# A kernel of four layers on one core: the expert part's gate multiplications spread one per step, and their tiles loaded on the weights' queue

## The chip, the cores and the metric

The kernel runs on one core of a Trainium2 chip. The time is what the device takes for one launch, in microseconds; of several runs the median counts. Lower is better.

## What is computed

Two blocks run one after the other on 256 tokens of width 1024. The first block has two layers of convolution, retention and window attention. The second has two layers of a mixer and a feed-forward part that looks up experts. The change lies in that last part alone, so only it is shown (the two layers are called layer 0 and layer 1 below):

```python
def block(t):
    q = (t @ w_pq).reshape(T, PEER_HEADS, 2, PEER_HALF)
    s = jnp.einsum('thpk,hpnk->thpn', q, sub_keys, ...)
    ...
    gate = jax.nn.softmax(best_s, axis=-1)
    u = expert_down[experts]
    act = jax.nn.gelu(jnp.einsum('td,thkd->thk', t, u, ...), approximate=False)
    wgt = (gate * act).astype(t.dtype)
    vv = expert_up[experts]
    return jnp.einsum('thk,thkd->td', wgt, vv)
```

There are 16384 experts, and each token uses 128 of them. The kernel does not gather. It multiplies the tokens with all experts, and the gate, which is zero for all others, picks.

## The kernel before

The experts are worked in 64 blocks `b2` of 256. For each, `down(b2, dst)` computes the activations of all tokens (16 key steps, three matmuls each, since every f32 operand is split in a high and a low part), and the loop `for b2 in range(64)` near the end of `peer` multiplies them with the rows of `up`: 24 matmuls of 128x512 (line 1184) for each step, summed over all steps in four PSUM banks, `accs`. I call one pass of that loop a step, and the loop the up part.

The weights of a step come as two halves. `half` (lines 100 to 115) loads each on SP's queue into one of four buffers `raw` (512 KB), ACT rounds it into `hi`, and DVE subtracts that, into `lo`; `hi` and `lo` have five buffers each. The activations of a step are split in the same way, into `wah` on ACT and `wal` on DVE, with two buffers each. So DVE has two `lo` and one `wal` for each step.

The gates come from an earlier loop. For the first 24 of 128 key columns (steps 0 to 11) they are multiplied there into `acti`. For the rest they are written to DRAM, `g_dram`, in 13 tiles of 1 MB; each serves four steps. `late(b2)` fetches a tile every fourth step, on ACT's queue, into one of two buffers `gt`, and multiplies the step's activations with it on DVE (line 1147). For steps 12 to 43 the activations lie ready in SBUF (`saved`: the tiles `uh`, `ul`, `xs`, `actl`); from step 44 on `late` also calls `down`, which loads 1 MB more and has 48 matmuls of 128x256. `late(b2 + AHEAD)`, with AHEAD = 2, stands in step `b2`.

Layer 0 also computes the modulation of the mixer that follows it, in units `ada`: a load of 256 KB on SP's queue into one of two buffers, and a multiplication with a sum on DVE (line 298), with a short addition (line 300). They begin at step 16. Seventeen have come due by then; after that there is one for each step, and four from step 44 on. Layer 1 has none.

The program text doesn't set the order on an engine. A scheduler does, by what it expects to be ready when, with the program's order and priorities; SP's queue, DVE, ACT and PE then each take their instructions strictly in that order. `tc.issue_after(x)` binds what a block issues on the engine of `x` to come behind `x` there.

Of the kernel before, what the change touches and what calls it, by code (L numbers as in the profile page):

```python
# [8 lines left out]
F32 = mybir.dt.float32  # L9
# [10 lines left out]
P = 128  # L20
T = 256
# [11 lines left out]
PEER_NS, PEER_NI, AHEAD = 44, 12, 2  # L33
# [17 lines left out]
def two_blocks_kernel(ctx: ExitStack, tc: tile.TileContext, ins: dict, out: bass.AP, stages=None):  # L51
    nc = tc.nc
# [30 lines left out]
    def nm(base):  # L83
        uid[0] += 1
        return f"{base}_{uid[0]}"

    def split(hi, lo, src):
        return nc.scalar.copy(hi, src), nc.vector.tensor_tensor(lo, src, hi.bitcast(F32), op=ALU.subtract)  # L88
# [4 lines left out]
    def bank(ring="mm", shape=(P, 2, T)):  # L93
        n = turns[ring] = turns.get(ring, -1) + 1
        b = BANKS[ring][n % len(BANKS[ring])]
        return psum.tile(list(shape), F32, tag=f"bank{b}", name=nm(ring))

    after = [None, None, 0]
    last_dma = [None]
# [14 lines left out]
    def slab(src):  # L114
        h = [half(src, i) for i in range(2)]
        return [[x[k] for x in h] for k in range(2)]
# [107 lines left out]
    def shift_bias(pb, pool, w, sh2):  # L224
        for ct in range(2):
            for kt in range(KT):
                for i in range(2):
                    nc.tensor.matmul(pb[0:2, 0, ct * P:(ct + 1) * P], sh2[:, kt, :], w[i][ct][:, kt * P:(kt + 1) * P],
                                     start=kt == 0 and i == 0, stop=kt == KT - 1 and i == 1)
        row = pool.tile([2, T], F32, tag="sbr", name=nm("sbr"))  # L230
        nc.scalar.copy(row, pb[0:2, 0, :])
        for ct in range(2):
            nc.tensor.matmul(pb[:, 1, ct:ct + 1], row[:, ct * P:(ct + 1) * P], ones_c[0:2, :], start=True, stop=True)
        b = pool.tile([P, 2], F32, tag="sb", name=nm("sb"))
        nc.vector.tensor_copy(b, pb[:, 1, 0:2])
        return b
# [17 lines left out]
    if stages_m:  # L254
        tb_dram = [drp.tile([P, 383], F32, tag=f"tb{h}", name=f"tb{h}") for h in range(8)]
        x_dram = [drp.tile([P, KT, T], F32, tag=f"xd{i}", name=f"xd{i}") for i in range(DEPTH)]
        g_dram = [drp.tile([13, P, T, 8], F32, tag=f"gd{i}", name=f"gd{i}") for i in range(DEPTH)]
# [24 lines left out]
    def ada_units(l, pool, tag, bufs, size, place=None):  # L282
        cact = []

        def load():
            cp, ct = place or (pool, "c_rows")
            cact.append(cp.tile([P, D], F32, tag=ct, name=nm("c_rows"), bufs=1))
            nc.sync.dma_start(cact[0], ins["c_rows"])
            nc.scalar.activation(cact[0], cact[0], AF.Silu)

        yield load
        for j in range(48):
            for c in range(0, D, size):
                def unit(j=j, c=c):
                    w = pool.tile([P, size], F32, tag=tag, name=nm("ada"), bufs=bufs)
                    nc.sync.dma_start(w, ins["w_ada"][l, j, :, c:c + size])
                    t = pool.tile([P, 1], F32, tag="adt", name=nm("adt"))
                    nc.vector.scalar_tensor_tensor(w, w, 1.0, cact[0][:, c:c + size], op0=ALU.mult, op1=ALU.mult,  # L298
                                                   accum_out=t)
                    nc.vector.tensor_tensor(mods[l][:, j:j + 1], mods[l][:, j:j + 1], t, op=ALU.add)  # L300
                yield unit
# [648 lines left out]
    def peer(l, uu, follow):  # L950
        NS, NI = PEER_NS, PEER_NI
        GS = 2 * NI
        NGR = (P - GS) // 8
        with ExitStack() as bx:
# [13 lines left out]
            def down(b2, dst):  # L968
                w = slab(ins["down"][l, b2])
                ps = bank("pm")  # L970
                mm_T(ps, w, hh)
                nc.scalar.activation(dst, ps, AF.Gelu)  # L972

            with ExitStack() as tx:
# [14 lines left out]
                with tc.tile_pool(name=f"tt{l}", bufs=2) as tq:  # L989
                    for h in range(8):  # L990
                        w = slab(ins["w_pq"][l, h])
                        qT = tq.tile([P, 2, T], F32, tag="qT", name=nm("qT"))
                        if h < PEER_U:
                            pb = bank("pb")
                            b = shift_bias(pb, tq, w, shifts["p", l])
# [36 lines left out]
                def saved(i):  # L1032
                    t, k = (spare[i // 4], i % 4) if i < 12 else (actl, i - 12)
                    return t[:, 2 * k:2 * k + 2, :]
# [57 lines left out]
            wu = bx.enter_context(tc.tile_pool(name=f"up{l}", bufs=2))  # L1092
# [37 lines left out]
                    nc.scalar.dma_start(g_dram[l][:NGR, :, t0:t0 + 16, :].rearrange("g p t b -> p g t b"), stg)  # L1130

            accs = [bank("acc", (P, 512)) for _ in range(4)]
            gtile = None
            wa_q = {}

            def late(b2):
                nonlocal gtile
                if b2 < NS:
                    wa = saved(b2 - NI)
                else:  # L1140
                    wa = wu.tile([P, 2, T], F32, tag="ua", name=nm("wa"), bufs=4)
                    down(b2, wa)
                if (2 * b2 - GS) % 8 == 0:
                    gtile = wu.tile([P, T, 8], F32, tag="gt", name=nm("gt"), bufs=2)
                    nc.scalar.dma_start(gtile, g_dram[l][(2 * b2 - GS) // 8])
                g = gtile[:, :, 2 * b2 % 8:2 * b2 % 8 + 2].rearrange("p t b -> p b t")
                nc.vector.tensor_tensor(wa, wa, g, op=ALU.mult)  # L1147
                wa_q[b2] = wa

            units = ada[follow[1]] if follow else []  # L1150
            credit, pace = 0, None
            for b2 in range(64):
                if follow and b2 == NI + 4:
                    units.extend(ada_units(follow[1], wu, "ud", 2, 512, (upool, "uh")))
                credit += PEER_ADA[b2 >= NS]
                while units and credit >= 1:
                    credit -= 1
                    with ExitStack() as es:
                        if PACE and pace:
                            es.enter_context(tc.issue_after(pace.ins))  # L1160
                        if PACE > 1:
                            es.enter_context(tc.issue_after(last_dma[0].ins))
                        units.pop(0)()
                if b2 == NS:
                    X[0] = glob.tile([P, KT, T], F32, tag="xT", name=nm("xT"))
                    for k2 in range(KT // 2):
                        nc.sync.dma_start(X[0][:, 2 * k2:2 * k2 + 2, :], x_dram[l][:, 2 * k2:2 * k2 + 2, :])
                for b in range(NI, 64) if b2 == 0 else ():
                    if b < AHEAD:
                        late(b)  # L1170
                if NI <= b2 + AHEAD < 64:
                    late(b2 + AHEAD)
                wa = acti[:, 2 * b2:2 * b2 + 2, :] if b2 < NI else wa_q.pop(b2)
                uh, ul = slab(ins["up"][l, b2])
                wah = wu.tile([P, 2, T], F32R, tag="ub", name=nm("wah"), bufs=2)
                wal = wu.tile([P, 2, T], F32R, tag="uc", name=nm("wal"), bufs=2)
                pace = split(wah, wal, wa)[1]
                for k in range(2):
                    first, end = b2 == 0 and k == 0, b2 == 63 and k == 1
                    for tt in range(2):  # L1180
                        tsl = slice(tt * P, (tt + 1) * P)
                        for lh, rh, i in ((wah, uh, 0), (wah, ul, 1), (wal, uh, 2)):
                            for n in range(2):
                                nc.tensor.matmul(accs[2 * tt + n], lh[:, k, tsl],  # L1184
                                                     rh[k][:, n * 512:(n + 1) * 512],
                                                     start=first and i == 0, stop=end and i == 2)
# [18 lines left out]
    for i in range(nh, len(stages)):  # L1205
        k, l = stages[i]
        u = (mix if k == "m" else peer)(l, u, follows[i])
# [147 lines left out]
```

## Time and profile before

| | |
|---|---|
| Median of 3 runs | 3028.61 us (3024.74 to 3031.89) |
| The profiled execution's own time | 3032.76 us |
| Its span in the profile | 3030.4 us |
| PE busy | 2939.5 us, 97% of the span |
| DVE busy | 2418.9 us, 80% |
| ACT busy | 1521.7 us, 50% |
| Moved by DMA | 598.59 MB, mean 198 GB/s |
| Up part of layer 0, first to last 128x512 matmul | from 1562.2 us, some 490 us |
| Up part of layer 1 | from 2549.1 to 3021 us |

The profile is of one execution. Matmuls overlap in their pipeline, so that "PE busy" reaches 100% wherever they follow each other without a gap, and gaps are better seen by counting the matmuls of a stretch. A wait is put down to the instruction whose signal came last.

### The profile page before, as it was taken

To read this page: it belongs to the slowest core of one execution; us is meant where nothing else is said; L and a number is where in the kernel's file an instruction comes from. 1 tells how busy PE (TensorE), PEld (TensorE's weight loads), DVE (VectorE), ACT (ScalarE), POOL (GpSimd) and SP (SyncE) were. 2 spreads that over 40 slices of the span, in tenths; PEclk is the share of its full clock that TensorE was granted. 3 is DMA by queue.
4 is the path that set the end of the run, shared out by engine and by line. 5 is a ranking of instruction groups with operands and counts; after the bars stand their busy time and mean duration, and the time that the engine had idled before them with its cause. 6 is when DMAs were issued, how large, how long until landed. Compare 5 with 4: busy or idle time off the path is not lost.

```text
span 3030.4 us, 55658 instructions
## 1 busy us (share of the span) xinstructions
PE 2939.5 (97%) x21784; PEld 2726.1 (90%) x21784; DVE 2418.9 (80%) x5084; ACT 1521.7 (50%) x2113; POOL 76.3 (3%) x92
## 2 busy tenths in 40 slices
PE   8999999999999998999999899999999999999999
PEld 7889999988999997999987689888899999788998
DVE  7899988888898676999878767767699997855565
ACT  5664535565454554555544444445355444444443
POOL 0000000000000000000000000000000000000000
PEclk8999999999999999999999999999899999999999
DMA  6357448434745552556677878864255677765664
GB/s 205 123 181 265 165 161 278 162 124 161 241 168 169 175 165 93 178 178 208 214 244 275 274 242 273 279 221 152 84 169 182 202 218 238 272 208 194 204 218 136
DMA packets 227065, 598.59 MB, mean 198 GB/s; under 512 B 24881, under 2 KB 85841, under 8 KB 223473
## 3 DMA queue, kind: packets, MB, share of 16 engines
q1 hardware_dynamic: 160080, 533.63, 52.9%
q10 hardware_dynamic: 66720, 61.39, 6.3%
q8 instruction: 171, 2.80, 0.4%
q14 instruction: 94, 0.76, 0.1%
HBM read 562.97 MB, written 31.98 MB: 196 GB/s over the span
## 4 chain that ended last, share of the span: by engine, by line
PE 61%; DVE 6%; DMA 6%; issue 2%; ACT 1%; ACTq 0%; DVEq 0%
PE acc L1184 15%; PE pm L125 8%; PE pm L126 8%; PE pm L127 8%; DMA ada<-in_w_ada_dram 4%; PE mm L125 3%; PE mm L127 3%; PE g L1119 3%; PE mm L126 3%; DVE lo L88 2%; DVE actl L1147 1%; PE mm L137 1%; PE mm L136 1%; DVE ada L298 1%; PE mm L135 1%
## 5 line engine op out<-in xcount | busy, mean ns | idle before, releaser
L88 ACT CAST hi<-raw 128x1024 fp32r<-128x1024 f32 x904 | 946.6, 1050 | 993.6 <-PE pm L126 251.6
L88 DVE TENSOR_TENSOR lo<-raw,hi 128x1024 fp32r<-128x1024 f32 x904 | 1115.5, 1237 | 303.2 <-ACT hi L88 300.2
L125 PE MATMUL pm<-h_hi,hi 128*128 128x256 f32 x2272 | 642.2, 283 | 10.8 <-ACT acti L972 7.7
L126 PE MATMUL pm<-h_lo,hi 128*128 128x256 f32 x2272 | 640.4, 282 | 4.5 <-DVE h_lo L219 4.5
L127 PE MATMUL pm<-h_hi,lo 128*128 128x256 f32 x2272 | 639.9, 282 | 2.9 <-DVE lo L88 2.9
L125 PEld LDWEIGHTS pm<-h_hi,hi 128*128 128x128 f32 x2272 | 430.1, 189 | 13.2 <-ACT acti L972 8.1
L126 PEld LDWEIGHTS pm<-h_lo,hi 128*128 128x128 f32 x2272 | 430.2, 189 | 6.4 <-DVE h_lo L219 4.9
L127 PEld LDWEIGHTS pm<-h_hi,lo 128*128 128x128 f32 x2272 | 430.1, 189 | 3.6 <-DVE lo L88 3.5
L125 PE MATMUL mm<-h_hi,hi 128*128 128x256 f32 x1472 | 419.5, 285 | 0.0
L126 PE MATMUL mm<-h_lo,hi 128*128 128x256 f32 x1472 | 416.0, 283 | 0.0
L127 PE MATMUL mm<-h_hi,lo 128*128 128x256 f32 x1472 | 415.6, 282 | 0.0
L1184 PE MATMUL acc<-hi,wal 128*128 128x512 f32 x1024 | 318.7, 394 | 25.5 <-DVE wal L88 25.5
L1184 PE MATMUL acc<-lo,wah 128*128 128x512 f32 x1024 | 318.0, 391 | 3.9 <-DVE lo L88 3.9
L1184 PE MATMUL acc<-hi,wah 128*128 128x512 f32 x1024 | 317.7, 392 | 0.0
L125 PEld LDWEIGHTS mm<-h_hi,hi 128*128 128x128 f32 x1472 | 278.5, 189 | 8.9 <-issue 8.3
L126 PEld LDWEIGHTS mm<-h_lo,hi 128*128 128x128 f32 x1472 | 278.6, 189 | 6.2 <-issue 6.1
L127 PEld LDWEIGHTS mm<-h_hi,lo 128*128 128x128 f32 x1472 | 278.3, 189 | 5.6 <-issue 5.6
L1184 PEld LDWEIGHTS acc<-hi,wal 128*128 128x128 f32 x1024 | 191.9, 189 | 73.4 <-DVE wal L88 33.9
L420 DVE SCALAR_TENSOR_TENSOR conv<-cv,conv_dw,conv 128x256 f32<-128x256 f32 x480 | 241.0, 512 | 3.3
L1184 PEld LDWEIGHTS acc<-lo,wah 128*128 128x128 f32 x1024 | 192.8, 189 | 46.4 <-DVE lo L88 5.6
L1184 PEld LDWEIGHTS acc<-hi,wah 128*128 128x128 f32 x1024 | 190.4, 189 | 38.1 <-ACT wah L88 0.3
L298 DVE SCALAR_TENSOR_TENSOR ada<-ada,c_rows 128x512 f32<-128x512 f32 (+1 forms) x144 | 126.2, 881 | 77.4 <-DMA ada<-in_w_ada_dram 71.9
(400 smaller groups left out, 4731.7 us busy)
## 6 DMA issues: line engine op xcount, KB each, us to landing
raw<-in_w_in_dram SPq DMA_DIRECT2D x264, 512.0 KB, 4.1
raw<-in_down_dram SPq DMA_DIRECT2D x256, 512.0 KB, 4.3
raw<-in_up_dram SPq DMA_DIRECT2D x256, 512.0 KB, 4.6
gd<-stg ACTq DMA_DIRECT2D x32, 832.0 KB, 5.0
gt<-gd ACTq DMA_DIRECT2D x26, 1024.0 KB, 6.7
ada<-in_w_ada_dram SPq DMA_DIRECT2D x48, 512.0 KB, 4.9
ada<-in_w_ada_dram SPq DMA_DIRECT2D x96, 256.0 KB, 4.2
raw<-in_w_ret_out_dram SPq DMA_DIRECT2D x32, 512.0 KB, 3.6
```

The costliest lines, as they stand in the source:

```text
L88: return nc.scalar.copy(hi, src), nc.vector.tensor_tensor(lo, src, hi.bitcast(F32), op=ALU.subtract)
L125: nc.tensor.matmul(ps[:, ct, :], wh[:, kt, c], ah[:, kt, :], start=s, stop=False)
L126: nc.tensor.matmul(ps[:, ct, :], wh[:, kt, c], al[:, kt, :], start=False, stop=False)
L127: nc.tensor.matmul(ps[:, ct, :], wl[:, kt, c], ah[:, kt, :], start=False, stop=e)
L135: nc.tensor.matmul(ps[:, tt, :], ah[:, kt, c], wh[:, kt % 4, :], start=kt == 0, stop=False)
L136: nc.tensor.matmul(ps[:, tt, :], ah[:, kt, c], wl[:, kt % 4, :], start=False, stop=False)
L137: nc.tensor.matmul(ps[:, tt, :], al[:, kt, c], wh[:, kt % 4, :], start=False, stop=kt == KT - 1)
L298: nc.vector.scalar_tensor_tensor(w, w, 1.0, cact[0][:, c:c + size], op0=ALU.mult, op1=ALU.mult, accum_out=t)
L420: nc.vector.scalar_tensor_tensor(a, v[:, k:k + T], dw[:, c, k:k + 1], a, op0=ALU.mult, op1=ALU.add)
L1119: nc.tensor.matmul(pg[:, k, :], oh[0][:, j // 2, :, j % 2], oh[2 + i][:, j // 2, :, j % 2], start=i == 0, stop=i == 2)
L1147: nc.vector.tensor_tensor(wa, wa, g, op=ALU.mult)
L1184: nc.tensor.matmul(accs[2 * tt + n], lh[:, k, tsl], rh[k][:, n * 512:(n + 1) * 512], start=first and i == 0, stop=end and i == 2)
```

## The change

Three things. The gate tiles are loaded by `gate_columns(n)` on SP's queue, tied behind the load of the half before it; tile n is asked for in step 8 + 4n, four steps ahead of the first step that needs it. The multiplication of step `b2 + 2` is tied on DVE behind the `wal` of step `b2 - 1`. The loop `for b in range(NI, 64) if b2 == 0`, which did nothing with these constants, is gone.

```diff
             accs = [bank("acc", (P, 512)) for _ in range(4)]
-            gtile = None
+            gtiles = {}
             wa_q = {}
 
+            def gate_columns(n):
+                gtiles[n] = wu.tile([P, T, 8], F32, tag="gt", name=nm("gt"), bufs=2)
+                nc.sync.dma_start(gtiles[n], g_dram[l][n])
+
             def late(b2):
-                nonlocal gtile
                 if b2 < NS:
                     wa = saved(b2 - NI)
                 else:
                     wa = wu.tile([P, 2, T], F32, tag="ua", name=nm("wa"), bufs=4)
                     down(b2, wa)
-                if (2 * b2 - GS) % 8 == 0:
-                    gtile = wu.tile([P, T, 8], F32, tag="gt", name=nm("gt"), bufs=2)
-                    nc.scalar.dma_start(gtile, g_dram[l][(2 * b2 - GS) // 8])
-                g = gtile[:, :, 2 * b2 % 8:2 * b2 % 8 + 2].rearrange("p t b -> p b t")
+                g = gtiles[(2 * b2 - GS) // 8][:, :, 2 * b2 % 8:2 * b2 % 8 + 2].rearrange("p t b -> p b t")
                 nc.vector.tensor_tensor(wa, wa, g, op=ALU.mult)
                 wa_q[b2] = wa
...
-                for b in range(NI, 64) if b2 == 0 else ():
-                    if b < AHEAD:
-                        late(b)
+                n, c = divmod(2 * (b2 + AHEAD + 2) - GS, 8)
+                if b2 and 0 <= n < NGR and c == 0:
+                    with tc.issue_after(last_dma[0].ins):
+                        gate_columns(n)
                 if NI <= b2 + AHEAD < 64:
-                    late(b2 + AHEAD)
+                    with tc.issue_after(wsplit.ins):
+                        late(b2 + AHEAD)
...
-                pace = split(wah, wal, wa)[1]
+                wsplit = pace = split(wah, wal, wa)[1]
```

What it moves is seen in the order of each engine. On DVE, in layer 0, before, the stretch that begins with the `lo` of step 2 (L1147 is a gate multiplication, `x4` four of them in a row; `uh` and `ul` are the saved activations of steps 12 to 15 and 16 to 19; `wal_19805` is step 2's and `wal_19845` step 3's):

```order
L88 TENSOR_TENSOR lo_19794<-raw_19792,hi_19793 128x1024
L88 TENSOR_TENSOR lo_19800<-raw_19798,hi_19799 128x1024
L1147 TENSOR_TENSOR uh_15557<-uh_15557,gt_20112 128x512 x4
L88 TENSOR_TENSOR wal_19805<-acti_14594,wah_19804 128x512
L88 TENSOR_TENSOR lo_19834<-raw_19832,hi_19833 128x1024
L1147 TENSOR_TENSOR ul_15558<-ul_15558,gt_20278 128x512 x4
L88 TENSOR_TENSOR lo_19840<-raw_19838,hi_19839 128x1024
L88 TENSOR_TENSOR wal_19845<-acti_14594,wah_19844 128x512
```

Now the first of these multiplications stands behind the `wal` of step 9, and the same four rows repeat to step 15 (layer 1: to step 41):

```order
L88 TENSOR_TENSOR wal_20087<-acti_14594,wah_20086 128x512
L1147 TENSOR_TENSOR uh_15557<-uh_15557,gt_20032 128x512
L88 TENSOR_TENSOR lo_20117<-raw_20115,hi_20116 128x1024
L88 TENSOR_TENSOR lo_20123<-raw_20121,hi_20122 128x1024
L88 TENSOR_TENSOR wal_20128<-acti_14594,wah_20127 128x512
L1147 TENSOR_TENSOR uh_15557<-uh_15557,gt_20032 128x512
```

In both layers the 32 multiplications of steps 12 to 43, which stood in groups of one to four ahead of the `wal` of steps 2 to 10, stand one per step behind the `wal` of steps 9 to 40; all of them now leave the first nine steps free.

On SP's queue, in layer 0, the stretch of steps 19 to 21 before (`raw` from `in_up` are the halves of the up weights, `ada` the units):

```order
L296 DMA ada_20385<-in_w_ada_dram 128x512
L105 DMA raw_20592<-in_up_dram 128x1024
L296 DMA ada_20390<-in_w_ada_dram 128x512
L296 DMA ada_20395<-in_w_ada_dram 128x512
L105 DMA raw_20632<-in_up_dram 128x1024
L296 DMA ada_20400<-in_w_ada_dram 128x512
L105 DMA raw_20638<-in_up_dram 128x1024
L296 DMA ada_20405<-in_w_ada_dram 128x512
L296 DMA ada_20410<-in_w_ada_dram 128x512
```

And now:

```order
L296 DMA ada_20385<-in_w_ada_dram 128x512
L105 DMA raw_20592<-in_up_dram 128x1024
L1138 DMA gt_20631<-gd_100 128x2048
L296 DMA ada_20390<-in_w_ada_dram 128x512
L105 DMA raw_20634<-in_up_dram 128x1024
L296 DMA ada_20395<-in_w_ada_dram 128x512
L105 DMA raw_20640<-in_up_dram 128x1024
L105 DMA raw_20680<-in_up_dram 128x1024
L296 DMA ada_20400<-in_w_ada_dram 128x512
```

A gate tile stands behind the halves of every fourth step (7, 11, 15, ... 55), and the units are spaced wider: ten steps from step 18 on had 26 of them and the ten after that 10; now they have 18 and 18. From step 41 on the units and the halves of `down` lie nearly as before. PE's order is the same in all but a few places, where matmuls of one step change places. On DVE, between the first unit and step 35, a step now has one multiplication, two `lo`, one `wal` and one to three units, where before there were two `lo`, one `wal` and two to three units, then one.

## Rows read from the trace of the kernel before

**Rows 1.** The page's first part: busy time and share of each engine.

```profile
PE 2939.5 (97%) x21784; PEld 2726.1 (90%) x21784; DVE 2418.9 (80%) x5084; ACT 1521.7 (50%) x2113; POOL 76.3 (3%) x92
```

**Rows 2.** PE's waits: engine, line, releaser, us in total, times, longest.

```profile
PE acc L1184 <- DVE wal L88: 25.5, 20, 2.8
...
PE acc L1184 <- DVE lo L88: 3.9, 4, 1.5
```

**Rows 3.** Line 1184 alone, layer 0: stretch, length, PE, PEld busy (count), clock, DMA, GB/s.

```profile
1660.00:1740.00 80.00, 70.56 (x289) 55.62 (x288) 0.96 0.80 267
1740.00:1800.00 60.00, 60.00 (x266) 49.67 (x265) 1.00 0.75 243
1562.00:1642.00 80.00, 70.92 (x302) 56.12 (x303) 1.00 0.81 285
```

**Rows 4.** The same in layer 1.

```profile
2560.00:2620.00 60.00, 51.85 (x214) 40.33 (x213) 0.97 0.80 279
...
2700.00:2760.00 60.00, 60.00 (x266) 49.70 (x265) 1.00 0.59 193
```

**Rows 5.** Timeline, layer 0, step 2: start, us, engine, line, idle before and releaser.

```profile
1571.32 4.28 DVE L1147 TENSOR_TENSOR uh<-uh,gt 128x512 f32<-128x512 f32 x4 [2.39 <-DMA gt<-gd]
...
1575.50 0.69 DVE L88 TENSOR_TENSOR wal<-acti,wah 128x512 fp32r<-128x512 f32 x1
...
1576.10 1.23 DVE L88 TENSOR_TENSOR lo<-raw,hi 128x1024 fp32r<-128x1024 f32 x1
...
1576.25 1.21 PE L1184 MATMUL acc<-hi,wal 128*128 128x512 f32 x4 [1.14 <-DVE wal L88]
1577.00 0.62 ACT L88 CAST wah<-acti 128x512 fp32r<-128x512 f32 x1
...
1577.24 4.40 DVE L1147 TENSOR_TENSOR ul<-ul,gt 128x512 f32<-128x512 f32 x4
```

**Rows 6.** All engines: stretch, length, busy of PE, PEld, DVE, ACT, POOL, clock, DMA, GB/s.

```profile
1560.00:1640.00 80.00, 71.14 (x315) 56.53 (x314) 67.45 (x68) 30.07 (x36) 0.00 (x0) 1.00 0.81 287
1660.00:1722.00 62.00, 52.56 (x210) 40.73 (x208) 45.28 (x103) 25.13 (x31) 0.00 (x0) 0.94 0.77 257
...
1740.00:1800.00 60.00, 60.00 (x266) 49.67 (x265) 41.42 (x68) 28.90 (x33) 0.00 (x0) 1.00 0.75 243
1820.00:1980.00 160.00, 154.18 (x989) 139.23 (x988) 120.57 (x237) 71.23 (x84) 0.00 (x0) 1.00 0.82 276
```

**Rows 7.** DVE's timeline in layer 0, the units of two steps.

```profile
1669.03 0.69 DVE L298 SCALAR_TENSOR_TENSOR ada<-ada,c_rows 128x512 f32<-128x512 f32 x1 [2.38 <-DMA ada<-in_w_ada_dram]
1669.64 0.08 DVE L298 DVE_READ_ACCUMULATOR ada<-ada,c_rows 128x1 f32 x1
1669.64 1.22 DVE L88 TENSOR_TENSOR lo<-raw,hi 128x1024 fp32r<-128x1024 f32 x1
1670.78 0.15 DVE L300 TENSOR_TENSOR mod<-mod,adt 128x1 f32<-128x1 f32 x1
...
1676.35 0.69 DVE L298 SCALAR_TENSOR_TENSOR ada<-ada,c_rows 128x512 f32<-128x512 f32 x1 [1.94 <-DMA ada<-in_w_ada_dram]
```

**Rows 8.** Waits between 1660 and 1722 us, the burst of units in layer 0.

```profile
DVE ada L298 <- DMA ada<-in_w_ada_dram: 16.3, 15, 2.4
...
PE acc L1184 <- DVE wal L88: 9.4, 7, 2.8
```

**Rows 9.** DMA issues from 1660 us: queue, count, KB each, median us to landing.

```profile
ada<-in_w_ada_dram SPq DMA_DIRECT2D x27, 256.0 KB, 4.2
```

**Rows 10.** The same from 1740 to 1800 us, then from 1840 to 1960 us.

```profile
ada<-in_w_ada_dram SPq DMA_DIRECT2D x11, 256.0 KB, 3.4
...
ada<-in_w_ada_dram SPq DMA_DIRECT2D x40, 256.0 KB, 4.5
...
gt<-gd ACTq DMA_DIRECT2D x2, 1024.0 KB, 8.0
```

**Rows 11.** Waits between 1900 and 1980 us in layer 0, with `down` in every step.

```profile
PE acc L1184 <- DVE lo L88: 2.9, 2, 1.5
PE pm L127 <- DVE lo L88: 2.9, 2, 1.6
```

## The prediction

> **What bounds the kernel now.** I read the shares of the engines first. PE is busy for 97% of the span, DVE for 80% [rows 1]. So the kernel is bound by PE nearly everywhere, and a change off PE can only win what PE loses to waits. I then read PE's waits. The longest sum belongs to the line this change is about: the matmuls of the up part waited 25.5 us in 20 places for DVE's `wal` [rows 2]. This understates the loss, because a matmul's modelled end overlaps the gap behind it. To see it whole I counted matmuls by stretch. Undisturbed, 266 of line 1184 fall into 60 us [rows 3, 4], that is 60 / 266 = 0.2256 us each. A step of 24 takes 5.4 us. At this pace 80 us hold 354.7. Three stretches fall short:
>
> - Layer 0, first 80 us of the up part: 302 [rows 3]; 52.7 are missing, times 0.2256 = 11.9 us.
> - Layer 1, 2560 to 2620 us: 214 of 266 [rows 4]; 52 missing, 11.7 us. The granted clock is 0.97 here, and its cost is in this count.
> - Layer 0, 1660 to 1740 us: 289 [rows 3]; 65.7 missing, 14.8 us.
>
> The timeline shows the reason for the first two. DVE does four gate multiplications in a row (4.28 us, after 2.39 us of waiting for the gate tile), and only then the `wal` that PE needs; PE stands until that is done [rows 5]. The third is another matter: no gate multiplication is left there. It is the burst of `ada` units, where DVE waits 16.3 us in 15 places for the units' loads and passes 9.4 us of that on to PE [rows 8].
>
> **The gates leave steps 2 to 10.** 32 multiplications in each layer are moved, not removed. One costs 4.28 / 4 = 1.07 us [rows 5]. In layer 1 the new place is free. DVE's work in a step is two `lo` at some 1.14 us (1669.64 to 1670.78 [rows 7]), a `wal` at 0.60 (1575.50 to 1576.10 [rows 5]) and one gate at 1.07, together 3.95 of 5.4 us. What covers it is PE's own step. The `wal` of a step can be made once PE is through with the step two before it, takes 0.62 us on ACT and 0.69 on DVE [rows 5], and is needed 5.4 us after that moment: 4.1 us of slack. The gate stands behind it and takes from the next `lo`. Were the slack gone, each gate would cost PE 1.07 us. The tiles add 1.049 MB for each four steps, 0.262 a step, to 1.049 MB of weights. There is a stretch with this traffic: from 1740 to 1800 us in layer 0 one unit of 0.262 MB goes with each step on the same queue, at 243 GB/s, and PE misses nothing [rows 3, 6]. The buffer of tile n was last read by the gate behind the `wal` of step 4n + 4, and SP comes to tile n only when the `lo` of step 4n + 5 has freed the raw buffer of the half ahead, so SP doesn't stand there. Removing ACT's wait for a free `gt` buffer costs nothing. I take both early stretches as won, less 0.5 us each for a first fill: -11.4 and -11.2, **-22.6 us** together. The bounds are the whole counts (-23.6), and half of them (-11.8) if the `lo` become late instead.
>
> **Layer 0, the units.** Here the change brings load into a busy stretch. On SP's queue, steps 18 to 37 held 40 halves (20.97 MB), 36 units (9.44) and the four loads of `xT` (1.05); now five gate tiles (5.24) come with them, 36.7 MB in all. In 20 steps of 5.44 us, 108.8 us, that asks for 337 GB/s. The stretches with a full queue reached 257, 276 and 287 GB/s at DMA shares of 0.77 to 0.82 [rows 6]; 257 is from the burst itself, where the units' two buffers held the queue back (26 units in ten steps). Units are now spread, 18 and 18 for ten steps each, so the buffers matter less. I take 290, near the upper row: 126.6 us, 17.8 over the steps' own time, less the 4.1 of slack, gives 13.7 us lost. Now 14.8 are lost there, so the difference is -1.1, which I round to 0: the burst goes, a shortage of bandwidth comes. Bounds: at 276 GB/s 133.0 us, 20.1 lost, **+5.3**; at 318 (the 243 of the quiet row, which had a share of 0.75, carried to a share of 0.98) 115.4 us, 2.5 lost, **-12.3**.
>
> DVE says the same from its side. With 1.8 units to a step, each 0.61 (1669.03 to 1669.64) and some 0.07 for the addition, its work there is 3.95 + 1.8 x 0.68 = 5.2 of 5.4 us. There is 0.2 us a step to take up any wait for a unit. A unit lands 4.2 us after its issue in the burst, 3.4 in the quiet stretch, 4.5 in the late one [rows 9, 10]; from one unit to the next in the same buffer DVE has some 4.6 us of other work between (two `lo`, a `wal`, a gate and a unit). A landing of 5 us is already felt at every unit.
>
> **Layer 0, from step 44.** `down` joins, the order is nearly as before, but the tiles come on SP's queue, and four instead of three fall here. The stretch runs at 276 GB/s and loses some PE time to late `lo`: the waits are 2.9 + 2.9 us [rows 11], and a tile on ACT's queue took 8.0 us to land [rows 10]. One more tile is 1.049 / 0.276 = 3.8 us of transfer; half of it I take as hidden by the loads that run ahead: **+1.9 us** (bounds -2, if the weights run further ahead, and +6, if all of it and a wait of 1.5 us show).
>
> **The rest.** PE's order changes within a step only, and the loop that goes did nothing: 0. In layer 1 the late part misses no matmul now and asks for less: 0.
>
> **Sum.** -22.6 + 0 + 1.9 = -20.7 us. From the profiled execution's 3032.76 this gives 3012.1. The median of the runs shown is 3028.61, 4.15 lower, so I forecast **3008 us** for the median.
>
> **Rivals.**
>
> *The gain of layer 0 is given back.* The shared queue runs no faster with the tiles in it than the two stretches with units do, 257 to 276 GB/s. At 276 the stretch costs +5.3, at 257 (142.8 us, 29.9 lost) +15.1, and the late part +4 with either, as it starts with less loaded ahead: -13.3 to -3.5, 3015 to 3025 us. For it speaks that DVE is nearly full; against it that the row with gate tiles and weights alone reached 287. Chance 0.17.
>
> *The burst dissolves altogether.* If the wider spacing of the units alone cures the stretch, 2.5 us are lost there and the late part costs nothing: -22.6 - 12.3 = -34.9, about 2994 us; half that way is 3001. Chance 0.15.
>
> *Slower: a tile stands in front of the units on the one queue.* Ten tiles (steps 19 to 55) now precede units on SP's queue. DVE waits for the unit behind the tile, and the `wal` and both `lo` wait behind that. If PE pays a tile's whole landing each time, 8.0 us [rows 10], it is 80 us against the 14.8 + 5.8 now lost in these stretches: +59.4 - 22.6 = +36.8, 3065 us. It decides from (20.6 + 22.6 + 6.1) / 10 = 4.9 us for a tile. Against it: the transfer itself takes only 1.049 / 0.287 = 3.7 us, the order leaves some 7.4 us for the unit behind a tile (three `lo`, two `wal`, two gates, one unit), and slack takes part. Chance 0.05. The Trainium skill has a rule that speaks for this rival ("DMA: Bandwidth & Descriptors", section "Queues, rings and completion order"): each DMA engine changes between the queues that have work packet by packet, but takes one queue's descriptors in their order. By that rule a tile on ACT's queue shares with the units, and on SP's queue goes wholly ahead of them. No row here shows a tile on SP's queue. By the rule with 3.7 us a tile and no slack, ten would cost 37 us, and the sum would be 37 - 20.6 - 22.6 = -6.2, 3022 us; this milder form is counted with the first rival.
>
> *The gates are not the reason.* The early waits could be the `hi` and `lo` that aren't far enough ahead when the up part begins; then DVE's gates only filled time, and the waits move to `lo`: about 3028 us. For it: PE waits there for a `lo` too (3.9 us in the whole run [rows 2]). Against it: each gap ends with a `wal` that stood behind gates. Chance 0.03.
>
> **How the numbers follow.** The forecast has the remaining 0.60. The range reaches from the half-way case of the dissolved burst, with the bound of -23.6 and the late part at its best, to most of the first rival: 2996 to 3022 us. A change of under 0.2%, 6.1 us, can't be told from none here. Faster means under 3022.5: all of the forecast and of the dissolved burst, and 0.12 of the first rival: 0.87. Same: the rest of that rival and the last one: 0.08. Slower: the tile in front of the units: 0.05.
>
> **What would show it.** Right: in layer 1, 2560 to 2620 us holds 264 to 266 matmuls of line 1184, at a clock of 1.00; PE's sum of waits for `wal` falls from 25.5 to about 10 us, all in layer 0 after the units begin; the DMA rate in layer 0 is some 230 GB/s up to step 18 and 290 from there to step 37. Wrong: `wal` or `lo` waits in layer 1; a DMA rate under 270 GB/s with DVE waiting on units in most steps; gaps on PE after each tile of layer 0.

## The result, and the profile after

| | time, median | runs | lowest to highest |
|---|---|---|---|
| before | 3026.68 us | 6 | 3021.56 to 3034.65 |
| changed | 2998.82 us | 6 | 2993.42 to 3006.20 |

The ratio is 0.990, with an interval from 0.9887 to 0.9913: 27.9 us faster, where 20.7 were forecast. The time lies within the range, near its lower end, 9 us under the 3008 that the sum gave.

The profiled execution took 3006.2 us (the highest of the six), with a span of 3004.3. The shares of the engines, against [rows 1]:

```profile
PE 2936.9 (98%) x21784; PEld 2728.8 (91%) x21784; DVE 2421.5 (81%) x5084; ACT 1523.1 (51%) x2113; POOL 76.2 (3%) x92
```

Nobody has less work; DVE's 2421.5 us even are 2.6 more. What changed is PE's waits (engine, line, releaser, us in total, times, longest), against [rows 2]; line 1184 is 1186 now:

```profile
PE acc L1186 <- DVE wal L88: 4.7, 7, 1.5
PE acc L1186 <- DVE lo L88: 3.9, 2, 3.3
```

25.5 us in 20 places have become 4.7 in 7, all seven between 1660 and 1790 us in layer 0. The line's matmuls by stretch (columns as in [rows 3]), first layer 0, then layer 1:

```profile
1566.00:1646.00 80.00, 79.46 (x351) 65.92 (x352) 1.00 0.72 238
...
1664.00:1744.00 80.00, 77.13 (x334) 61.91 (x334) 1.00 0.91 325
```

```profile
2560.00:2620.00 60.00, 60.00 (x267) 49.67 (x266) 1.00 0.72 248
```

The first stretch has 351 matmuls where [rows 3] had 302, the one in layer 1 has 267 where [rows 4] had 214, at a clock of 1.00. The stretch with the units has 334 where it had 289: better, but still 20 short of the 354.7 that PE could do. All engines in the two long stretches with units (columns as in [rows 6]):

```profile
1660.00:1780.00 120.00, 115.21 (x498) 92.43 (x497) 108.96 (x190) 53.51 (x62) 0.00 (x0) 1.00 0.90 312
1820.00:1980.00 160.00, 154.73 (x976) 138.77 (x975) 122.81 (x231) 70.36 (x84) 0.00 (x0) 0.99 0.83 279
```

The DMA moves 312 GB/s at a share of 0.90 there. The forecast had put 290.

To compare kernels step by step, I read from PE's trace when each step of the up part starts, counting 24 matmuls of the line to a step (each trace has all 1536 of a layer). A column runs from the start of one step to the start of another. "Turn" is from the last pair of matmuls of layer 0's up part to the first matmul of layer 1's, and "whole" from there to its last pair. Each row is one execution. Times in us:

| kernel | layer 0, steps 0 to 16 | 16 to 41 | 41 to 63 | turn | layer 1, whole |
|---|---|---|---|---|---|
| before | 98.4 | 150.9 | 239.8 | 492.7 | 472.2 |
| changed | 87.1 | 143.5 | 241.5 | 491.9 | 460.3 |
| e1_pace_only | 87.1 | 146.3 | 240.7 | 492.7 | 460.3 |
| e2_load_only | 92.6 | 156.2 | 239.7 | 493.0 | 473.2 |
| e4_after_smooth | 87.1 | 136.0 | 239.8 | 496.9 | 460.3 |
| e5_before_smooth | 100.0 | 136.0 | 237.3 | 493.6 | 472.6 |
| e6_half_sum | 87.1 | 141.4 | 232.8 | 489.7 | 460.3 |
| e7_half_load | 87.1 | 145.4 | 238.4 | 490.8 | 460.3 |
| e8_smooth_early | 87.1 | 138.5 | 239.5 | 492.7 | 460.3 |
| e9_three_bufs | 87.1 | 136.0 | 232.2 | 492.2 | 460.3 |
| e10_after_three | 87.1 | 137.9 | 232.2 | 494.2 | 460.3 |
| e11_before_three | 99.1 | 140.4 | 232.2 | 492.7 | 471.8 |

Layer 1, which has no units, shows in the changed kernel what an undisturbed pass takes: 87.1, 136.0 and 232.2 us. So the change won 11.3 us in layer 0's first steps, 11.9 in layer 1 and 7.4 in the units' stretch, and lost 1.7 late: 28.9 us in sum, near the 27.9 between the medians. (The spans of the two profiled executions differ by 26.1, as the up part of the changed one began 4.3 us later; the change edits nothing ahead of it.) Of layer 0's loss, 7.5 us in steps 16 to 41 and 9.3 after them were left. The expectations quoted below were written from an earlier reading of these starts that is off by up to a microsecond: where they have 144.0, 8.0, 14.3 and 8, the table gives 143.5, 7.5, 14.9 and, for the late loss of the kernel before, 7.6.

### The profile page after: what moved, and what is told of

It is laid out like the page before. It is cut to its first block, busy times and chain, and to the rows that moved or that the text cites. A ratio compares the mean times of both kernels' runs of the same rounds, so it can differ in the third digit from the quotient of the medians.

```text
span 3004.3 us, 55646 instructions
## 1 busy us (share of the span) xinstructions
PE 2936.9 (98%) x21784; PEld 2728.8 (91%) x21784; DVE 2421.5 (81%) x5084; ACT 1523.1 (51%) x2113; POOL 76.2 (3%) x92
## 4 chain that ended last, share of the span: by engine, by line
PE 63%; DMA 6%; DVE 5%; issue 2%; ACT 1%; DVEq 0%; ACTq 0%
PE acc L1186 17%; PE pm L125 8%; PE pm L126 8%; PE pm L127 8%; DMA ada<-in_w_ada_dram 5%; PE g L1119 3%; PE mm L125 3%; PE mm L127 3%; PE mm L126 3%; DVE lo L88 1%; DVE ada L298 1%; PE mm L136 1%; PE mm L137 1%; PE mm L135 1%; PE tr L144 1%
## 5 line engine op out<-in xcount | busy, mean ns | idle before, releaser
L125 PEld LDWEIGHTS pm<-h_hi,hi 128*128 128x128 f32 x2272 | 430.0, 189 | 11.9 <-ACT acti L972 6.8
```

What stands on the lines that cost most here:

```text
L125: nc.tensor.matmul(ps[:, ct, :], wh[:, kt, c], ah[:, kt, :], start=s, stop=False)
```

## The experiments

Two questions: which of the change's two parts makes the gain, and what holds the units' stretch. My leading theory at first was that the pacing makes the gain, wherever the tiles are loaded, and that the units' stretch is held by a DMA that is full.

### The pacing alone, the load alone

e1 is the kernel before with nothing but the tie. The tiles are still loaded on ACT's queue, inside `late`:

```diff
-                    late(b2 + AHEAD)
+                    with tc.issue_after(wsplit.ins):
+                        late(b2 + AHEAD)
```

> Pacing alone: the gate multiplications tied one per step behind the split before, the tiles still loaded in `late` on ACT's queue. Theory A (DVE's place for the multiplications is what was won, the queue of the tiles hardly matters): both early stretches miss no matmul, layer 1's up part takes 460 us as with the whole change (before: 472), and the time is within 4 us of the whole change's, 2995 to 3003. Rival B (a tile ahead of the units on SP's queue costs PE time in the whole change): the late stretch of layer 0 loses 3 us or more less than the whole change's some 8, and the time is 2992 to 2996. Rival C (a load on ACT's queue that waits for a free buffer holds up the `hi` behind it, and that was part of the early loss): 5 us or more slower than the whole change, 3004 or above.

Measured: 3004.03 us (6 runs), ratio 0.9906 [0.9888, 0.9924]. Both early stretches are won in full, and PE's waits are like those of the changed kernel:

```profile
PE acc L1185 <- DVE wal L88: 6.7, 6, 1.8
PE acc L1185 <- DVE lo L88: 1.2, 1, 1.2
```

The time is 1 us above what the leading theory allowed, and touches Rival C's bound; but the early loss that Rival C speaks of isn't there, and the interval overlaps that of the whole change, so the tiles' queue makes no difference that these runs can tell. In layer 1 there is none at all: 460.3 us with either. Rival B fails too: the late steps lose 0.8 us less than with the whole change, not 3.

e2 is the changed kernel without the tie: the tiles are loaded ahead on SP's queue, and the scheduler puts the multiplications where it likes.

```diff
-                    with tc.issue_after(wsplit.ins):
-                        late(b2 + AHEAD)
+                    late(b2 + AHEAD)
```

> Loading ahead alone: the tiles on SP's queue as in the whole change, the multiplications not tied. The order has them in twos in layer 1 and in fours in layer 0's units stretch, ahead of the step's `wal`. Theory A (a step has 4.1 us of slack, so what must not happen is a group that uses it up): layer 1 as with the whole change, 460 us, since two take 2.14 us; layer 0 loses 3 to 8 us more than the whole change in the units stretch, where four take 4.28 us on a DVE that is nearly full: 3002 to 3007. Rival D (it is the load's new time that spreads the work, the tie is worth nothing): within 2 us of the whole change, 2997 to 3001. Rival E (any group ahead of `wal` costs PE about what it did before): 10 us or more slower than the whole change, with `wal` waits in layer 1 too.

Measured: 3027.94 us (12 runs), ratio 0.9998 [0.9982, 1.0013]. The load ahead alone gives nothing. My leading theory (3002 to 3007) missed by over 20 us; the numbers are Rival E's, with PE waiting for `wal` in layer 1 too (8.2 us in 5 places). The early stretches do not stay as they were either: the loss moves. In layer 1 it is now 4.0 us in steps 0 to 16 and 8.9 in steps 16 to 41, where before all 11.9 lay in the first. DVE's waits in layer 1, 2541 to 2800 us:

```profile
DVE actl L1147 <- DMA gt<-gd: 21.1, 5, 5.2
DVE xs L1147 <- DMA gt<-gd: 6.2, 1, 6.2
```

The timeline around one of them (columns as in [rows 5]), in step 14 of layer 1:

```profile
2612.40 0.62 ACT L88 CAST wah<-uh 128x512 fp32r<-128x512 f32 x1 [1.07 <-PE acc L1185]
...
2618.76 2.11 DVE L1147 TENSOR_TENSOR xs<-xs,gt 128x512 f32<-128x512 f32 x2 [6.18 <-DMA gt<-gd]
...
2620.79 0.68 DVE L88 TENSOR_TENSOR wal<-uh,wah 128x512 fp32r<-128x512 f32 x1
...
2621.53 0.73 PE L1185 MATMUL acc<-hi,wal 128*128 128x512 f32 x2 [2.14 <-DVE wal L88]
```

DVE stands 6.18 us for the tile, then makes two multiplications, and only then the `wal` that PE wants. `wah` was there at 2613.02; the `wal` begins 7.8 us after it. Here the early load with no tie left the consumers in groups ahead of the `wal`, and they outran the tile's landing; layer 1 lost as much as before (12.9 us, where it was 11.9). So of the change's two parts the tie is the one that pays.

### The units' stretch: how fast are they asked for?

In e4 and e5 the units come due evenly: no unit is owed when they begin, and then 1 a step and 3.5 from step 44 on. Fewer bytes are asked for in the stretch. e4 does this to the changed kernel, e5 to the one before.

```diff
-PEER_ADA = (1, 4)
+PEER_ADA = (1, 3.5)
...
+                    credit = 0
                     units.extend(ada_units(follow[1], wu, "ud", 2, 512, (upool, "uh")))
```

> The whole change, and the units' saved-up credit of 17 dropped at step 16; one unit per step, then 3.5 from step 44 on (they end at step 63 in place of 57). Theory A (what PE still loses in layer 0 is units and tiles together asking for more than the DMA gives, 337 GB/s asked and some 315 given): with one unit a step 289 GB/s are asked up to step 43 and 297 after, the units stretch loses under 2 us (now 7 to 8) and the late one under 4 (now about 8): 2986 to 2991. Rival F (the losses come from a tile standing ahead of a unit on one queue, whatever the rate): the tiles still stand there, and the losses stay: 2996 to 3001.

Measured: 2994.3 us (4 runs), ratio 0.9883 [0.9862, 0.9905]. The stretch's loss is gone, 136.0 us, with the tiles where they were, so Rival F fails there. The time still misses the expected 2986 to 2991: 7.6 us remain late, where under 4 were expected, and the turn costs 5 more (496.9), as the last units now end with the up part.

> The kernel before with the units' credit dropped in the same way and nothing else. Theory A (the third stretch, 14.8 us, is the burst of units and independent of the gates): layer 0 from 1660 to 1740 us misses at most 2 us, the early stretches stay as they were (some 11.5 us each in layers 0 and 1), the late one loses 0 to 4: 3007 to 3014. Rival G (part of the third stretch is an echo of the early one, weights not far enough ahead): 3018 to 3023.

Measured: 3016.74 us (5 runs), ratio 0.9956 [0.994, 0.9973]. The time misses the expected 3007 to 3014 by 3 us, as the late steps still lose 5.1. But the third stretch of the kernel before loses nothing any more, and the two early ones stay. So the third loss is the units' alone, and has nothing to do with the gates.

e8 is e4 with the units a little earlier, `PEER_ADA = (1.25, 3.6)`, so that the turn is left free.

> The whole change with the units evenly spread as in the run before, but at 1.25 a step up to step 43 and 3.6 after, so that they end at step 60 and not in the last step. Theory A: 301 GB/s are asked up to step 43, under the 312 seen, so steps 16 to 41 take 136 to 138 us; the step from the up part of layer 0 to that of layer 1 is back at 492 us (it was 497 where units ran to the last step), and the time is 3 to 6 us under that run: 2988 to 2992. Rival F' (any more units per step bring the losses back): steps 16 to 41 at 140 us or more, 2994 or above.

Measured: 2992.97 us (4 runs), ratio 0.9884 [0.9868, 0.99]. The turn is free (492.7), but 2.5 us come back in the stretch, between the two expectations, and the late loss stays (7.3): no better than e4.

### The units' stretch: the queue's rate, or DVE?

e6 and e7 are the changed kernel with one half of a unit taken away. In e6 the multiplication on DVE covers 256 of the 512 columns, the load is whole; in e7 the load brings 256 columns, and the multiplication reads them twice.

```diff
-                    nc.vector.scalar_tensor_tensor(w, w, 1.0, cact[0][:, c:c + size], ...
+                    q = size // 2 if size == 512 else size
+                    nc.vector.scalar_tensor_tensor(w[:, :q], w[:, :q], 1.0, cact[0][:, c:c + q], ...
```

> The whole change, and each unit of layer 0's up part multiplies and sums only half of its 512 columns (the other half of the modulation's sums is left out); the loads stay whole. The question is what costs the 8.0 us that PE still loses between steps 16 and 41 (144.0 us in place of 136.0). DVE's work in a step falls there from 5.2 to about 4.7 of 5.44 us; the bytes asked for stay. Theory A (the DMA is at its limit, 337 GB/s asked, 312 given): the loss stays at 5 us or more, steps 16 to 41 take 141 us or more. Rival H (DVE is full and has no time left for waits): 136 to 139 us.

Measured, one execution: 2987.06 us. Steps 16 to 41 lose 5.4 us instead of 7.5, at 320 GB/s, and the late steps almost nothing. The loss that stays in the stretch spoke for the DMA's rate; that the late one goes spoke for DVE.

```diff
-                    nc.sync.dma_start(w, ins["w_ada"][l, j, :, c:c + size])
+                    nc.sync.dma_start(w[:, :q], ins["w_ada"][l, j, :, c:c + q])
```

> The counterpart: each unit of layer 0's up part loads only half of its bytes and reads them twice (the sums are those of the first half taken with both halves of the condition); DVE's work for a unit stays. The scheduler answers with more units per step (some 2.3, so DVE's work is 5.5 of 5.44 us from step 16 to 28), and 315 GB/s are asked there in place of 337. Theory A: 136 to 140 us for steps 16 to 41. Rival H (DVE is the limit): DVE has more to do in these steps than in the whole change, 143 us or more.

Measured, one execution: 3000.07 us. The leading theory expected 136 to 140 us for steps 16 to 41, its rival 143 or more; it was 145.4. All engines there:

```profile
1660.00:1780.00 120.00, 112.82 (x490) 91.08 (x489) 108.36 (x189) 55.15 (x64) 0.00 (x0) 1.00 0.81 281
```

The DMA moves only 281 GB/s, and the loss is larger than in the changed kernel (9.4 us). But the scheduler had packed the shorter units closer, so two things changed in this kernel; I take from it only that a full DMA is not needed for the loss.

### The third buffer

What the two halves have in common is the time from a unit's issue to its use. A unit's load goes out when the unit two before it is done. With 1.8 units to a step of 5.44 us, that is 2 x 3.02 us ahead of its turn, less the 0.69 of the multiplication: 5.3 us, an estimate from [rows 7] and the step. The loads' landing in the changed kernel, 1660 to 1780 us (columns as in [rows 9]):

```profile
ada<-in_w_ada_dram SPq DMA_DIRECT2D x35, 256.0 KB, 5.3
gt<-gd SPq DMA_DIRECT2D x5, 1024.0 KB, 8.3
```

The median is all the time that there is, so many units come too late. The chain of work that ended last shows the same. Of its longest pieces (start, us, what), one unit's load after another stands in the burst; between them lie shorter pieces of other work, and units' loads come again after 1850 us:

```profile
1566.70 75.76 PE acc L1186 x334
...
1680.53 4.80 DMA ada<-in_w_ada_dram
1686.08 6.84 DMA ada<-in_w_ada_dram
1699.23 6.70 DMA ada<-in_w_ada_dram
1710.18 7.19 DMA ada<-in_w_ada_dram
1729.06 8.14 DMA ada<-in_w_ada_dram
1737.94 5.34 DMA ada<-in_w_ada_dram
1745.99 5.32 DMA ada<-in_w_ada_dram
1755.66 6.89 DMA ada<-in_w_ada_dram
1765.27 37.49 PE acc L1186 x164
```

A third buffer gives another 3.02 us. e9 adds it to e8, e10 to the changed kernel and e11 to the kernel before:

```diff
-                       for g, b in (("ua", 4), ("ua", 4), ("ub", 2), ("uc", 2), ("ud", 2))]
+                       for g, b in (("ua", 4), ("ua", 4), ("ub", 2), ("uc", 2), ("ud", 3))]
...
-                    units.extend(ada_units(follow[1], wu, "ud", 2, 512, (upool, "uh")))
+                    units.extend(ada_units(follow[1], wu, "ud", 3, 512, (upool, "uh")))
```

(The first line is an earlier loop that has its tiles in the same memory.)

> The same with three buffers for the units in place of two. In the run before this one with units evenly spread, DVE still waited 55.7 us in 23 places for units from step 41 on, and PE lost 5.7 us there. If it is the two buffers (a load goes out only when the unit two before it is done): the waits of DVE for units fall under 15 us and PE's loss between steps 41 and 63 under 3 us, 2985 to 2989. Rival (the loads are late because the DMA is full, 300 GB/s asked): the loss stays within 2 us of the two-buffer kernel.

Measured: 2987.47 us (4 runs), ratio 0.986 [0.9841, 0.988]. Layer 0's up part takes as long as layer 1's, 460.3 us: no loss is left, at 323 GB/s, and DVE's waits for units after step 41 are 12.3 us, under the 15 expected.

But e9 also spreads the units. e10 has the whole burst, and the third buffer alone:

> The changed kernel with a third buffer for the units' loads and nothing else; the units come due as in the changed kernel (about 337 GB/s asked for in steps 18 to 37). What is still lost in layer 0 (8.0 us in steps 16 to 41, 8 to 9 us after step 41) is here put to the test. Theory of the two buffers (a unit's load goes out only when the unit two before it is done, so its landing of 5 us is waited for on DVE): both losses fall, steps 16 to 41 take 136 to 140 us, the steps from 41 to 63 no more than 236, the waits of DVE for units between 1660 and 2045 us fall to a third or less, and the time is 2982 to 2990 us (ratio to the kernel before 0.984 to 0.988). Theory of the DMA's rate (the stretch asks for more than is moved): steps 16 to 41 keep a loss of 6 us or more at 310 to 325 GB/s, only the late part gains, and the time is 2991 to 2999 us.

Measured: 2986.83 us (5 runs), ratio 0.9863 [0.9844, 0.9883]. The two stretches, to be held against those of the changed kernel above:

```profile
1660.00:1780.00 120.00, 119.39 (x523) 97.37 (x522) 113.81 (x198) 57.84 (x68) 0.00 (x0) 1.00 0.94 338
1820.00:1980.00 160.00, 160.00 (x1047) 146.31 (x1046) 124.76 (x226) 75.83 (x89) 0.00 (x0) 1.00 0.83 285
```

It is again 35 units and five tiles, but 338 GB/s are moved where 312 were, and PE does 523 matmuls where it did 498. The units take even longer to land, and nobody waits for that. Of e10, the loads' landing and DVE's wait for the units (1655 to 1790 us):

```profile
ada<-in_w_ada_dram SPq DMA_DIRECT2D x35, 256.0 KB, 5.8
```

```profile
DVE ada L298 <- DMA ada<-in_w_ada_dram: 1.8, 3, 0.9
```

In the changed kernel the same wait is

```profile
DVE ada L298 <- DMA ada<-in_w_ada_dram: 10.4, 12, 2.4
```

So the theory of the full DMA, mine to this point, falls: steps 16 to 41 lose 1.9 us, and the steps after them nothing. The rate was low because two buffers asked for no more. e10 stands where e9 does, so with three buffers the spreading adds nothing.

One part of the expectation failed. From 1655 to 2045 us DVE's waits for units were to fall to a third; they fell from 51.2 us to 32.3, and after 1790 us only from 40.8 to 30.5. The late loss of PE went all the same. What also fell is ACT's wait for the weights over the same time, first in the changed kernel, then in e10:

```profile
ACT hi L88 <- DMA raw<-in_up_dram: 85.8, 59, 4.7
```

```profile
ACT hi L88 <- DMA raw<-in_up_dram: 45.7, 37, 3.6
```

The weights' halves stand behind the units on SP's queue, and there a unit's load that waits for its buffer holds them up too: after 1790 us SP stood 62.1 us for the units' buffers (7.4 at most) in the changed kernel, 43.7 (5.2) in e10. With the third buffer the scheduler also orders DVE and the queue differently in places. So the buffer is the cause, but in the late steps the runs don't separate DVE's shorter waits, the earlier weights and the other order.

> The kernel before with a third buffer for the units' loads and nothing else: the gate multiplications still stand ahead of the wal of steps 2 to 10. Theory of the two buffers: the two early stretches stay as they are (23.6 us lost), the loss of 14.3 us in steps 16 to 41 of layer 0 and of 8 us after it fall to a third or less, and the time is 3004 to 3014 us. Theory of the crowded order (26 units in ten steps are more than DVE and the queue can take, with however many buffers): the third stretch loses 9 us or more, and the time is 3017 us or more. Either way the first 16 steps of both layers take 10 to 13 us longer than in the changed kernel, so the gain of the change and the gain of the buffer add up.

Measured: 3013.68 us (6 runs), ratio 0.9953 [0.9936, 0.9971]. The third stretch loses 4.4 us instead of 14.9, the late one nothing, and the early ones stay. Between e11 and e10 lie 26.9 us, between before and changed 27.9: the buffer and the change add up. e10 (or e9) is the version to keep, some 40 us faster than the kernel before.

## Why the prediction was right, and where it was not

**The gates leave steps 2 to 10: right, in place and size.** Forecast were -11.4 and -11.2 us; measured -11.3 and -11.9. Both layers now take the undisturbed 87.1 us for their first 16 steps, so the half us that I kept for a first fill was not needed. The slack of 4.1 us covered every paced multiplication in layer 1: no wait for `wal` is left there. e1 shows that the order on DVE is the cause, which disposes of the rival that the gates are not the reason.

**The units' stretch: the term that was mis-sized.** I put 0, with bounds of -12.3 and +5.3; it was -7.4, and that makes up most of the gap between the forecast and the result. The step that failed is "I take 290, near the upper row". It took the rates of [rows 6], 257 to 287 GB/s, for what the queue can carry. They were what was asked for: the queue carried 312 in the changed kernel, 323 in e9 and 338 in e10, which is the 337 that the text had worked out as the need. The rate alone does not give the size either: with 312 the same sum has 4.7 us lost, and 7.5 were. The second reading of the same place, from DVE's side, was the one to cost: "A landing of 5 us is already felt at every unit". It names the units' landing, and the first reading had named the two buffers; the runs with three buffers take nearly all of the loss away (1.9 us of 7.5 stay in e10, none in e9). I had both readings and made the sum from the wrong one.

**From step 44: +1.9 forecast, +1.7 measured (steps 41 to 63), but not by the means that I gave, so the fit is in part luck.** I had spread it as transfer time of one more tile. The changed kernel's timeline (columns as in [rows 5]) shows instead one large stop, while its other late stops are shorter than before (0.6 us at most, where the kernel before had four of 1.2 to 1.6):

```profile
1900.08 0.42 SPq L1138 DMA_DIRECT2D gt<-gd  x1
1900.91 1.41 SPq L296 DMA_DIRECT2D ada<-in_w_ada_dram  x2
...
1909.26 0.63 PE L1186 MATMUL acc<-hi,wah 128*128 128x512 f32 x2
1911.33 0.69 DVE L298 SCALAR_TENSOR_TENSOR ada<-ada,c_rows 128x512 f32<-128x512 f32 x1 [7.11 <-DMA ada<-in_w_ada_dram]
...
1911.95 1.22 DVE L88 TENSOR_TENSOR lo<-raw,hi 128x1024 fp32r<-128x1024 f32 x1
...
1913.22 0.78 PE L1186 MATMUL acc<-lo,wah 128*128 128x512 f32 x2 [3.34 <-DVE lo L88]
```

This is the rival of the tile in front of the units: the tile goes out, a unit behind it is late, DVE stands 7.11 us, the `lo` behind that is late, and PE stands 3.34. It happened, but of ten tiles only this one stopped PE for more than 1 us. The trace bears out only a part of the rule of the Trainium skill ("DMA: Bandwidth & Descriptors", section "Queues, rings and completion order") that one queue's descriptors are taken in their order, so that a tile goes ahead of the units. After the tiles at 1803, 1852, 1900 and 1951 us, DVE waited 4.5, 3.6, 7.1 and 4.7 us for a unit; no other late unit was waited for longer than 2.4. So on SP's queue a tile delays the next unit. After the three that e1 loads at about the times of the last three, on ACT's queue, it was 3.4, 4.3 and 3.8, where other units took up to 3.6, so there the tile can hardly be seen. The means of the three differ by 1.3 us, and most of that is the one wait of 7.1. In steps 18 to 37 no wait behind a tile is longer than 2.4 us, as the distance of 7.4 us that the text read from the order would lead one to expect. The price of 37 us by that rule is not seen.

**What should show it.** 264 to 266 matmuls in layer 1's 60 us: 267. Waits for `wal` of some 10 us, all in layer 0 behind the first unit: 4.7, all there. Some 230 GB/s, then 290: 238, then 312. The rival of the burst that dissolves was about half of what happened; with spread units it happens wholly (136.0 us), with the third buffer nearly (137.9).

**Open.** The rest of the late loss goes with the units' third buffer (e9 to e11), with the tiles where they were. In e10 DVE still waits 3.5 to 4.9 us behind each of the four late tiles, and PE doesn't stop, so a tile ahead of a unit is no loss by itself; which of the buffer's effects ends the stops isn't separated. How much of the 1.3 us is the queue and how much is chance of one execution each, wasn't tried. Nor was a version of e7 whose order stays as it is.

## What to carry to other kernels

On an engine that takes its work in order, work that is needed late belongs behind the work that is needed now, and a tie does that; here, loading earlier without a tie only let the scheduler move the wait. Before a DMA rate in a profile is taken as a limit, ask what could be asked for: in this kernel a load left as many units ahead of its use as there were buffers (an estimate of 5.3 us with two), and that was no longer than its landing (5.3 us), so the buffers were the limit. One buffer more is the cheap test.

## What I had not expected

The queue carried far more than any stretch of before shows. In e10 it carried 338 GB/s over 120 us, and PE lost almost nothing there. The DMA view of that stretch, in 40 slices of 3 us:

```profile
GB/s 372 400 395 371 252 348 235 307 378 391 397 314 294 376 408 425 397 397 379 335 287 274 351 387 385 365 288 262 289 406 391 345 248 302 230 302 400 324 233 259
```

The best slice has 425 GB/s, the worst 230. The Trainium skill ("DMA: Bandwidth & Descriptors", section "Specifications") gives about 358 GB/s as the limit of what a core gets from memory. The mean of the stretch is under that, but 19 of its slices are above, so here it is no cap on a few microseconds.

A short stop of PE can cost more than its length. After the 3.34 us from 1909.88 us on, the changed kernel's timeline of PE has the pairs of 128x512 matmuls like this:

```profile
1913.81 1.05 PE L1186 MATMUL acc<-hi,wal 128*128 128x512 f32 x2
1914.65 1.05 PE L1186 MATMUL acc<-hi,wah 128*128 128x512 f32 x2
1915.51 1.05 PE L1186 MATMUL acc<-lo,wah 128*128 128x512 f32 x2
1916.36 1.02 PE L1186 MATMUL acc<-hi,wal 128*128 128x512 f32 x2
1917.21 0.62 PE L1186 MATMUL acc<-hi,wah 128*128 128x512 f32 x2
1917.67 0.63 PE L1186 MATMUL acc<-lo,wah 128*128 128x512 f32 x2
```

A pair takes 0.85 us from start to start and 0.46 from 1917.21 on: the clock stood at the lower of its two levels, 1.2 GHz, for four pairs (the granted clock is 0.83 over 1909 to 1919 us, 0.66 over 1913 to 1918). At 0.39 us each this adds 1.6 us to a stop of 3.3. From 1660 to 1780 us, where no stop is longer than 1.5 us, the granted clock was 1.00.
